# First attention of a two-block kernel: probabilities kept whole, two heads' value products side by side on TensorE

## The chip, the cores and the metric

The kernel runs as one program on one core of a Trainium2 chip. The metric is the device time of one execution in microseconds, read as the median of several runs. The core has five engines, each with its own program: TensorE (PE in the rows; its weight loads are listed apart as PEld), VectorE (DVE), ScalarE (ACT), GpSimd (POOL) and SyncE (SP, which here only issues transfers). They wait for each other through semaphores.

## The reference, cut to what matters

The reference is two transformer-like blocks on 512 rows of width 1024, all in 32-bit floats. The change lies in the attention of the first block: 8 heads, 512 queries, 768 keys (256 context rows, then 512 rows of x), 96-wide queries and keys, 64-wide values.

```python
def attend(q_nope, q_rope, k_nope, k_rope, v):
    s = (jnp.einsum('bqhd,bkhd->bhqk', q_nope, k_nope)
         + jnp.einsum('bqhr,bkr->bhqk', q_rope, k_rope)).astype(jnp.float32) * SOFTMAX_SCALE
    p = jax.nn.softmax(s, axis=-1).astype(v.dtype)
    return jnp.einsum('bqhk,bkhd->bqhd', p, v)
...
def first_block(...):
    ...
    attn_l = attend_blocked(q_nope_l, q_rope_l, ...)      # attend, 128 queries at a time
    conv_l = conformer_conv(u_l, conv_dw_w[i], conv_dw_b[i], conv_ln_g[i], conv_ln_b[i])
    y_l = merge_groups(conv_l, attn_l, w_o[i], b_o[i])    # concat, then @ w_o + b_o
    x_mid = layer_norm(ALPHA * x + g1 * y_l, ln1_g[i], ln1_b[i])
    f_l = conv_ffn(x_mid * (1 + sc2) + sh2, w_up[i], ffn_dw_w[i], ffn_dw_b[i], w_down[i], b_down[i])
    x = layer_norm(ALPHA * x_mid + g2 * f_l, ln2_g[i], ln2_b[i])
```

The second block (sparse attention, a recurrent branch, a mixture of 64 experts) follows and is the larger part of the time; the change does not touch its code.

## The kernel before, in words

**Split products.** Most products take their operands as a pair: a rounded high part (a 32-bit type that TensorE takes in one go, `F32R` in the code) and the low rest. `evac` makes such a pair out of a PSUM bank: ScalarE copies the bank into the high part (L140), then VectorE subtracts that from the bank into the low part (L141), so the second waits for the first. `mm3` multiplies two pairs with three products (L85 high by high, L86 low by high, L87 high by low). Some products, those of the experts above all, take plain 32-bit operands (`F32`) in one instruction instead; the trace records each such instruction as two.

**Before the attention.** The key-value product (`ckh`, `ckl` by `wu`) makes keys and values for six tiles of 128 rows in the two large PSUM tiles (`dbank`). ScalarE copies the keys out, and `evac` writes the values as the pair `vh`, `vl`. The query product follows, with the depthwise convolution's taps (`conv`) on VectorE and GpSimd between.

**The attention.** `items` lists (head, tile of 128 queries), head by head, 32 in all. For each item, `scores` makes a 128 by 768 score tile with six products, takes the row maximum (VectorE, L670), the exponential with its row sum (ScalarE, L673), the reciprocal (VectorE, L674), and scales the probabilities `P` on GpSimd (L675). It runs two items ahead, one score tile in each of the two `dbank`. `turn` transposes `P` on TensorE (six products with the identity, L688) into two banks, of four and of two tiles, and `evac` writes each as a pair, `PTh` and `PTl`. `values` runs for every second item, on 256 queries of one head: for each of six key tiles an `mm3` of 128 value columns (this head's 64 and those of the head beside it) by the pair of probabilities, 18 products; of the 128 rows that come out, the 64 of this head are kept (`hp`). `keys` transposes a head's queries and keys and makes pairs of them, one head ahead. From item 23 on, steps of `conv_norm` (the convolution's layer norm and its transposes, which use the same four PSUM banks) are put between.

**Order.** In this part of the program a scheduler of the compiler orders each engine's instructions from its own estimate of times; the second block's experts have a fixed order on TensorE and SyncE.

Of the kernel before, what the change touches and what calls it, by code (L numbers as in the profile page):

```python
# [9 lines left out]
F32 = mybir.dt.float32  # L10
F32R = mybir.dt.float32r
# [3 lines left out]
AF = mybir.ActivationFunctionType  # L15
# [8 lines left out]
NT = S // 128  # L24
# [36 lines left out]
class Kernel:  # L61
# [276 lines left out]
    def block1(self):  # L338
        tc, nc, io = self.tc, self.nc, self.io
        v, act, pe, pool_e = nc.vector, nc.scalar, nc.tensor, nc.gpsimd  # L340
# [229 lines left out]
        pQ_cm, pQ = op("pQ", side="right")  # L570
        k96 = pQ.tile([128, 6, 8, 96], F32, name="k96")
        q96 = pQ.tile([128, NT, 8, 96], F32, name="q96")
        vh = pQ.tile([128, 6, 512], F32R, name="vh")
        vl = pQ.tile([128, 6, 512], F32R, name="vl")
        for t in range(6):
            pool_e.tensor_scalar(k96[:, t, :, 64:96], krow[:, t:t + 1, :].to_broadcast([128, 8, 32]), 1.0, 1.0,
                                 op0=ALU.mult, op1=ALU.mult)
# [1 line left out]
        for t in range(6):  # L579
            ps = self.dbank()  # L580
            sl = slice(t * 128, (t + 1) * 128)
            for h in range(2):
                for k in range(2):
                    self.mm3(ps[:, h * 512:(h + 1) * 512], (ckh[:, k, sl], ckl[:, k, sl]),
                             (wu[0][:, k, h * 512:(h + 1) * 512], wu[1][:, k, h * 512:(h + 1) * 512]), k == 0, k == 1)
            pr = ps.rearrange("p (h c) -> p h c", h=8)
            act.activation(k96[:, t, :, 0:64], pr[:, :, 0:64], AF.Copy)
            self.evac(vh[:, t, :].rearrange("p (h c) -> p h c", h=8), vl[:, t, :].rearrange("p (h c) -> p h c", h=8),
                      pr[:, :, 64:128])
            go(conv, 4)  # L590
        wuq = [self.wblock(io["w_uq"][0], 0, 3, h * 384, 384) for h in range(2)]
        for t in range(NT):
            sl = slice(t * 128, (t + 1) * 128)
            for h in range(2):
# [4 lines left out]
                pr = ps[:, :384].rearrange("p (h c) -> p h c", h=4)  # L599
# [10 lines left out]
        atth = pK.tile([128, 4, S], F32R, name="atth")  # L610
        attl = pK.tile([128, 4, S], F32R, name="attl")
        pH_cm, pH = op("pH", 2, side="right")
# [12 lines left out]
        def conv_norm():  # L625
            cnt = pH.tile([128, NT, 512], F32, name="cnt", tag="cnt", bufs=1)
            for t in range(NT):
                ps = self.bank()
                for c in range(4):
                    pe.transpose(ps[:, c * 128:(c + 1) * 128], cacc[:, c, t * 128:(t + 1) * 128], self.ident)  # L630
                s, b, _ = self.ln_stats([ps], LN_EPS)
                act.activation(cnt[:, t, :], ps, AF.Identity, bias=b, scale=s)
                yield
            for c in range(4):
                ps = self.bank()
                for t in range(NT):
                    pe.transpose(ps[:, t * 128:(t + 1) * 128], cnt[:, t, c * 128:(c + 1) * 128], self.ident)
                sl = pH.tile([128, S], F32, name="sl")
                act.activation(sl, ps, AF.Silu, bias=col["conv_ln_b"][:, c:c + 1], scale=col["conv_ln_g"][:, c:c + 1])
                self.split(cath[:, c, :], catl[:, c, :], sl)  # L640
                yield
        tail = conv_norm()
        items = [(h, t) for h in range(8) for t in range(NT)]
        QK, PT, Pt = {}, {}, {}

        def keys(h):
            r = []
            for src, name, n in ((q96, "q", 4), (k96, "k", 6)):
                hi = pH.tile([96, 128 * n], F32R, name=name + "Th")
                lo = pH.tile([96, 128 * n], F32R, name=name + "Tl")  # L650
                for g in range(0, n, 4):
                    m = min(4, n - g)
                    ps = self.bank()
                    for t in range(m):
                        pe.transpose(ps[:96, t * 128:(t + 1) * 128], src[:, g + t, h, :], self.ident)
                    self.evac(hi[:, g * 128:(g + m) * 128], lo[:, g * 128:(g + m) * 128], ps[:96, :m * 128])
                r.append((hi, lo))
            QK[h] = r

        def scores(i):  # L660
            if i >= len(items):
                return
            h, t = items[i]
            (qTh, qTl), (kTh, kTl) = QK[h]
            ps = self.dbank()
            qsl = slice(t * 128, (t + 1) * 128)
            for c0, c1 in ((0, 512), (512, 768)):
                self.mm3(ps[:, c0:c1], (qTh[:, qsl], qTl[:, qsl]), (kTh[:, c0:c1], kTl[:, c0:c1]), True, True)
            mx = self.small.tile([128, 3], F32, name="mx")
            v.tensor_reduce(mx[:, 0:1], ps[:, :768], axis=AX.X, op=ALU.max)  # L670
            v.tensor_scalar(mx[:, 0:1], mx[:, 0:1], -MLA_SCALE, None, op0=ALU.mult)
            P = pP.tile([128, 768], F32, name="P")
            act.activation(P, ps[:, :768], AF.Exp, bias=mx[:, 0:1], scale=MLA_SCALE, accum_out=mx[:, 1:2])  # L673
            v.reciprocal(mx[:, 2:3], mx[:, 1:2])  # L674
            pool_e.tensor_scalar(P, P, mx[:, 2:3], 1.0, op0=ALU.mult, op1=ALU.mult)  # L675
            Pt[i] = P

        def turn(i):
            h, t = items[i]
            if t % 2 == 0:  # L680
                PT[h, t // 2] = [pH.tile([128, 6, 256], F32R, name="PT" + x) for x in "hl"]
            PTh, PTl = PT[h, t // 2]
            P = Pt.pop(i)
            ql = slice((t % 2) * 128, (t % 2 + 1) * 128)
            for g, n in ((0, 4), (4, 2)):
                pt = self.bank()
                for j in range(n):
                    pe.transpose(pt[:, j * 128:(j + 1) * 128], P[:, (g + j) * 128:(g + j + 1) * 128], self.ident)  # L688
                self.evac(PTh[:, g:g + n, ql], PTl[:, g:g + n, ql], pt[:, :n * 128].rearrange("p (t c) -> p t c", t=n))

        def values(i):
            h, t = items[i]
            if t % 2 == 0:
                return
            PTh, PTl = PT.pop((h, t // 2))
            vs = slice((h // 2) * 128, (h // 2) * 128 + 128)
            hp = slice((h % 2) * 64, (h % 2) * 64 + 64)
            c = slice((t // 2) * 256, (t // 2 + 1) * 256)
            po = self.bank()
            for j in range(6):  # L700
                self.mm3(po[:, :256], (vh[:, j, vs], vl[:, j, vs]), (PTh[:, j, :], PTl[:, j, :]), j == 0, j == 5)
            self.evac(atth[hp, h // 2, c], attl[hp, h // 2, c], po[hp, :256])

        keys(0)
        for i in range(2):
            scores(i)
        for i in range(len(items)):
            h, t = items[i]
            if t == 0 and h < 7:
                keys(h + 1)  # L710
            scores(i + 2)
            turn(i)
            go(conv, 3)
            if i:
                values(i - 1)
            if i >= 23:
                go(tail, 1)
        values(len(items) - 1)
        self.dump2("cath", cath, catl)
        self.dump2("catA", atth, attl)  # L720
# [23 lines left out]
        for n in range(2):  # L744
            c = slice(n * 512, (n + 1) * 512)
# [22 lines left out]
        for t in range(NT):  # L768
# [5 lines left out]
            for n in range(2):  # L774
                c = slice(n * 512, (n + 1) * 512)
# [79 lines left out]
        for c in range(11):  # L855
# [5 lines left out]
            for mm in range(2):  # L861
                j = 2 * c + mm
# [7 lines left out]
        hh, hl = self.hh, self.hl  # L870
# [23 lines left out]
        for t in range(NT):  # L894
# [4 lines left out]
            for n in range(2):  # L899
                c = slice(n * 512, (n + 1) * 512)  # L900
# [1453 lines left out]
```

## Time and profile before

| | us |
|---|---|
| median of 3 runs (lowest, highest) | 2093.3 (2086.33, 2097.59) |
| the profiled execution's own time | 2086.47 |
| its span (first to last instruction) | 2084.7 |
| TensorE busy in the span | 1918.0 (92%) |
| attention, first transpose to the end of the last value product | 243.0 to about 357.3 |
| TensorE busy from 243 to 358 | 104.2 of 115 |

The profiled execution lies 6.8 us below the median of the runs. Busy time is the union of an engine's instructions; "granted clock" is the share of TensorE's full clock that the chip let through.

### The profile page before, as it was taken

The numbers are of one execution on the slowest core, as the hardware profiler recorded it, in microseconds if no ns is written. First come the engines' busy times: TensorE is split into PE (matmuls) and PEld (weight loads), VectorE is DVE, ScalarE is ACT, GpSimd is POOL, SyncE is SP. The second block draws the span as 40 slices with busy tenths as digits, with TensorE's granted clock in tenths as the row PEclk, the third lists the DMA queues.
The fourth block names the chain that finished last, engine by engine and source line by source line (L and its number), as shares of the span: only waits on it lengthen the run. The fifth ranks groups of instructions, "written<-read, shape, count | busy, mean of one in ns | idle before, by whom it ended". The sixth has DMA issues, their size and how long they took to land.

```text
span 2084.7 us, 30137 instructions
## 1 busy us (share of the span) xinstructions
PE 1918.0 (92%) x11420; PEld 1461.2 (70%) x11427; DVE 1175.3 (56%) x2137; ACT 661.3 (32%) x1168; POOL 555.2 (27%) x448
## 2 busy tenths in 40 slices
PE   4978898979999998997899999999899999999993
PEld 2657786777777887875677877788676666767662
DVE  4896576588574468565897576667332332222223
ACT  3213466434333325544323245523111111111111
POOL 1279422352012432012002100143122322223222
PEclk8989899989999999999799999999899999999997
DMA  8651102378462223549767631553999999999895
GB/s 284 215 185 60 51 1 78 110 253 296 141 208 97 101 91 115 153 127 236 223 177 177 170 114 62 172 166 133 358 327 360 306 381 329 354 362 336 316 367 173
DMA packets 208751, 425.47 MB, mean 204 GB/s; under 512 B 46694, under 2 KB 140280, under 8 KB 182485
## 3 DMA queue, kind: packets, MB, share of 16 engines
q1 hardware_dynamic: 184914, 366.98, 50.6%
q0 software_dynamic: 15488, 39.41, 7.7%
q10 hardware_dynamic: 8195, 17.06, 2.2%
q8 instruction: 92, 1.51, 0.3%
q14 instruction: 62, 0.51, 0.1%
HBM read 375.37 MB, written 60.08 MB: 209 GB/s over the span
## 4 chain that ended last, share of the span: by engine, by line
PE 70%; DVE 10%; DMA 7%; issue 5%; ACT 3%; POOL 3%; SPq 1%; POOLq 0%; ACTq 0%; DVEq 0%
PE bank L85 10%; PE bank L87 10%; PE bank L86 10%; PE gbank L2146 9%; PE wbank L2201 6%; PE bank L2132 3%; PE bank L2109 2%; PE gbank L2157 2%; PE dbank L85 2%; PE dbank L87 2%; PE dbank L86 2%; DVE cacc L486 1%; DMA ysum_db<-y,idxr 1%; DVE wlo L81 1%; PE wbank L2190 1%
## 5 line engine op out<-in xcount | busy, mean ns | idle before, releaser
L81 DVE TENSOR_TENSOR wlo<-raw,whi 128x1024 fp32r<-128x1024 f32 (+2 forms) x163 | 221.0, 1376 | 111.5 <-ACT whi L80 107.6
L85 PE MATMUL bank<-hh,whi 128*128 128x512 f32 (+3 forms) x720 | 273.2, 383 | 3.5 <-DVE hh L163 3.0
L86 PE MATMUL bank<-hl,whi 128*128 128x512 f32 (+3 forms) x720 | 273.4, 381 | 1.5 <-DVE hl L164 1.5
L87 PE MATMUL bank<-hh,wlo 128*128 128x512 f32 (+3 forms) x720 | 273.1, 382 | 1.0 <-DVE wlo L81 1.0
L80 ACT ACTIVATE whi<-raw 128x1024 fp32r<-128x1024 f32 (+2 forms) x163 | 161.7, 1025 | 241.9 <-PE bank L86 175.9
L2146 PE MATMUL gbank<-wr,xt 128*128 128x256 f32 x928 | 210.5, 385 | 0.9 <-issue 0.3
L2146 PEld LDWEIGHTS gbank<-wr,xt 128*128 128x128 f32 x928 | 175.7, 192 | 24.9 <-ACT xt L2115 1.0
L87 PEld LDWEIGHTS bank<-hh,wlo 128*128 128x128 f32 (+2 forms) x720 | 137.0, 191 | 35.3 <-issue 3.9
L85 PEld LDWEIGHTS bank<-hh,whi 128*128 128x128 f32 (+2 forms) x720 | 137.2, 192 | 32.1 <-DVE hh L163 3.4
L86 PEld LDWEIGHTS bank<-hl,whi 128*128 128x128 f32 (+2 forms) x720 | 137.7, 191 | 29.3 <-DVE hl L164 2.3
L2201 PE MATMUL wbank<-wr,ht 128*128 128x512 f32 (+2 forms) x456 | 138.7, 599 | 6.6 <-ACT ht L2173 5.6
L2162 DVE TENSOR_TENSOR h<-gbank,h 128x256 f32<-128x256 f32 (+1 forms) x40 | 17.0, 426 | 217.0 <-ACT h L2161 217.0
L2183 DVE SCALAR_TENSOR_TENSOR y<-wbank,wt,g2l 128x512 f32<-128x512 f32 (+1 forms) x69 | 51.7, 750 | 129.6 <-PE wbank L2201 110.3
L2201 PEld LDWEIGHTS wbank<-wr,ht 128*128 128x128 f32 (+2 forms) x456 | 51.2, 154 | 73.1 <-issue 62.8
L866 POOL TENSOR_TENSOR hid<-ug,uv 128x512 f32<-128x512 f32 x22 | 36.1, 1643 | 181.3 <-DVE uv L850 181.3
L486 DVE SCALAR_TENSOR_TENSOR cacc<-vpad,cols,cacc 128x512 f32<-128x512 f32 x90 | 83.6, 968 | 0.4
L2161 ACT ACTIVATE h<-gbank 128x256 f32<-128x256 f32 (+1 forms) x40 | 15.2, 381 | 210.8 <-PE gbank L2146 174.8
L2098 POOL DMA_INDIRECT xg<-h_d,idx x40 | 41.1, 1028 | 129.8 <-DVE idx L2093 80.2
L621 POOL TENSOR_TENSOR raw<-raw,g2row 128x2048 f32<-128x2048 f32 x11 | 55.0, 4999 | 73.8 <-DMA raw<-in_w_down_dram 73.5
L2132 PE MATMUL bank<-wr,xt 128*32 128x256 f32 (+1 forms) x896 | 65.9, 381 | 0.7 <-ACT xt L2115 0.2
L1990 POOL DMA_INDIRECT ysum_da<-y,idx x21 | 32.8, 1560 | 118.6 <-DVE y L2183 86.1
L2109 PEld LDWEIGHTS bank<-ident,xg 128*128 128x128 f32 (+1 forms) x392 | 48.8, 195 | 20.3 <-issue 15.3
(692 smaller groups left out, 4263.5 us busy)
## 6 DMA issues: line engine op xcount, KB each, us to landing
wr<-in_exp_gate_dram SPq DMA_DIRECT2D x52, 1024.0 KB
wr<-in_exp_up_dram SPq DMA_DIRECT2D x52, 1024.0 KB
wr<-in_exp_down_dram SPq DMA_DIRECT2D x52, 1024.0 KB
raw<-in_w_in_dram SPq DMA_DIRECT2D x58, 512.0 KB
mraw<-in_w_ada_dram SPq DMA_DIRECT2D x24, 1024.0 KB
mraw<-in_ada_w_dram SPq DMA_DIRECT2D x24, 1024.0 KB
raw<-in_w_up_dram SPq DMA_DIRECT2D x22, 1024.0 KB
raw<-in_w_down_dram SPq DMA_DIRECT2D x11, 1024.0 KB
```

Source lines behind the costliest of these rows:

```text
L80: self.nc.scalar.activation(hi, src, AF.Copy)
L81: self.nc.vector.tensor_tensor(lo, src, hi.bitcast(F32), op=ALU.subtract)
L85: mm(out, a[0], b[0], start=start, stop=False, skip_group_check=True)
L86: mm(out, a[0], b[1], start=False, stop=False, skip_group_check=True)
L87: mm(out, a[1], b[0], start=False, stop=stop, skip_group_check=True)
L486: eng.scalar_tensor_tensor(cacc[:, c, :], vpad[:, c, i:i + S], cw[:, i * 4 + c:i * 4 + c + 1], cacc[:, c, :], op0=ALU.mult, op1=ALU.add)
L621: return lambda raw, k, n: pool_e.tensor_tensor(raw, raw, row.unsqueeze(1).to_broadcast([128, k, n]), op=ALU.mult)
L2109: pe.transpose(ps[:, k * 128:k * 128 + r], x.rearrange("s (p k) -> s k p", k=8)[0:r, 4 * g + k, :], self.ident[0:r, 0:r])
L2132: pe.matmul(ps[to, 0:256], job.xt[:, k, sl], x[:, k * 256:(k + 1) * 256], start=k == 0, stop=k == 7, skip_group_check=True)
L2146: pe.matmul(ps[:, m * 256:(m + 1) * 256], job.xt[:, k, :], w[m][:, k * 256:(k + 1) * 256], start=k == 0, stop=k == 7, skip_group_check=True)
L2183: end = lambda c, ps: v.scalar_tensor_tensor(y[r, c], ps, job.wt[r], g2row[r, c], op0=ALU.mult, op1=ALU.mult)
L2201: pe.matmul(ps[to], job.ht[:, k, sl], x[:, k * D + c.start:k * D + c.stop], start=k == 0, stop=k == 1, skip_group_check=True)
```

## The change

The probabilities are no longer split. `turn` copies each transposed bank once into a 32-bit tile `PT`: ScalarE the bank of four tiles, VectorE the bank of two. The values stay whole too (`vals` in place of `vh`, `vl`, copied by VectorE alone). `items` now goes by pairs of heads: two query tiles of the even head, the same two of the odd head, then the other two of each. `values` runs once for a pair of heads and 256 queries: for each key tile one 32-bit product per head, in turns, with the even head's 64 value columns writing the result's rows 0 to 63 and the odd head's rows 64 to 127. One `evac` of 128 rows follows where there were two of 64. `keys` of the next two heads come at the fifth and seventh of a pair's eight items.

```diff
-        vh = pQ.tile([128, 6, 512], F32R, name="vh")
-        vl = pQ.tile([128, 6, 512], F32R, name="vl")
+        vals = pQ.tile([128, 6, 512], F32, name="vals")
...
-            self.evac(vh[:, t, :].rearrange("p (h c) -> p h c", h=8), vl[:, t, :].rearrange("p (h c) -> p h c", h=8),
-                      pr[:, :, 64:128])
+            v.tensor_copy(vals[:, t, :].rearrange("p (h c) -> p h c", h=8), pr[:, :, 64:128])
...
-        items = [(h, t) for h in range(8) for t in range(NT)]
+        items = [(2 * p + h, 2 * g + t) for p in range(4) for g in range(2) for h in range(2) for t in range(2)]
...
             if t % 2 == 0:
-                PT[h, t // 2] = [pH.tile([128, 6, 256], F32R, name="PT" + x) for x in "hl"]
-            PTh, PTl = PT[h, t // 2]
+                PT[h, t // 2] = pH.tile([128, 6, 256], F32, name="PT", bufs=4)
+            to = PT[h, t // 2]
...
-                self.evac(PTh[:, g:g + n, ql], PTl[:, g:g + n, ql], pt[:, :n * 128].rearrange("p (t c) -> p t c", t=n))
+                p3 = pt[:, :n * 128].rearrange("p (t c) -> p t c", t=n)
+                if g:
+                    v.tensor_copy(to[:, g:g + n, ql], p3)
+                else:
+                    act.activation(to[:, g:g + n, ql], p3, AF.Copy)
...
-            if t % 2 == 0:
+            if t % 2 == 0 or h % 2 == 0:
                 return
-            PTh, PTl = PT.pop((h, t // 2))
-            vs = slice((h // 2) * 128, (h // 2) * 128 + 128)
-            hp = slice((h % 2) * 64, (h % 2) * 64 + 64)
+            pair = [(x, PT.pop((x, t // 2)), slice((x % 2) * 64, (x % 2) * 64 + 64)) for x in (h - 1, h)]
             c = slice((t // 2) * 256, (t // 2 + 1) * 256)
             po = self.bank()
             for j in range(6):
-                self.mm3(po[:, :256], (vh[:, j, vs], vl[:, j, vs]), (PTh[:, j, :], PTl[:, j, :]), j == 0, j == 5)
-            self.evac(atth[hp, h // 2, c], attl[hp, h // 2, c], po[hp, :256])
+                for g, p, hp in pair:
+                    pe.matmul(po[hp, :256], vals[:, j, g * 64:(g + 1) * 64], p[:, j, :], start=j == 0, stop=j == 5,
+                              skip_group_check=True)
+            self.evac(atth[:, h // 2, c], attl[:, h // 2, c], po[:, :256])
...
+        keys(1)
         for i in range(len(items)):
-            h, t = items[i]
-            if t == 0 and h < 7:
-                keys(h + 1)
+            if i % 8 in (4, 6) and i < 24:
+                keys(2 * (i // 8) + 2 + (i % 8) // 6)
```

How the instructions move, on TensorE, at the first value product of before and the second of the changed kernel (numbers after names tell tiles apart). Before, after the last transposes of a turn:

```order
L688 MATMUL bank_1885<-ident_72,P_1817 128x128 x4
L688 MATMUL bank_1892<-ident_72,P_1817 128x128 x2
L85 MATMUL bank_1902<-PTh_1821,vh_1361 128x256
L86 MATMUL bank_1902<-PTl_1822,vh_1361 128x256
L87 MATMUL bank_1902<-PTh_1821,vl_1362 128x256
```

The three products come six times (18 rows). In the changed kernel, L687 is the transpose and L704 the value product:

```order
L687 MATMUL bank_2108<-ident_72,P_2044 128x128 x4
L687 MATMUL bank_2114<-ident_72,P_2044 128x128 x2
L704 MATMUL bank_2121<-PT_1953,vals_1361 64x256
L704 MATMUL bank_2121<-PT_2048,vals_1361 64x256
L704 MATMUL bank_2121<-PT_1953,vals_1361 64x256
```

The two heads' products alternate, 12 rows in all; there are 8 such groups where there were 16 of 18.

On VectorE, at the evacuation of the first values (L520 scales the latent rows `cn` of the last query tile, and waits for GpSimd), one piece of the difference:

```order
 L81 TENSOR_TENSOR wlo<-raw,whi 128x128
 L141 TENSOR_TENSOR cql<-bank,cqh 128x3x128
+L587 COPY vals<-dbank 128x512
 L520 SCALAR_TENSOR_TENSOR cn<-bank,ss,qg 128x384
-L141 TENSOR_TENSOR vl<-dbank,vh 128x512 x2
+L587 COPY vals<-dbank 128x512 x2
 L141 TENSOR_TENSOR cql<-bank,cqh 128x3x128
```

The first copy out of a `dbank` now stands ahead of `cn`, where both stood behind it.

On TensorE at the same place, before: the key-value product of the second tile ends, and the transposes of `cn` (L541) and a query product come next.

```order
L86 MATMUL dbank_1399<-wlo_1372,ckh_774 128x512
L87 MATMUL dbank_1399<-whi_1371,ckl_775 128x512
L541 MATMUL bank_1348<-ident_72,cn_1329 128x128 x3
L85 MATMUL bank_1525<-whi_1511,cqh_776 128x384
L86 MATMUL bank_1525<-wlo_1512,cqh_776 128x384
```

In the changed kernel the 12 products of the third tile (`dbank_1418`) come ahead of those transposes; the last three of them and what follows:

```order
L85 MATMUL dbank_1418<-whi_1370,ckh_774 128x512
L86 MATMUL dbank_1418<-wlo_1371,ckh_774 128x512
L87 MATMUL dbank_1418<-whi_1370,ckl_775 128x512
L541 MATMUL bank_1348<-ident_72,cn_1329 128x128 x3
L85 MATMUL bank_1518<-whi_1504,cqh_776 128x384
```

So the transposes of `cn` and the nine query products behind them moved back by one tile's 12 products. Smaller moves of the same kind go on through the rest of the first block, among them the order in which SyncE issues the loads of `w_up` and of the second block's `ada_w`.

## Rows read from the trace of the kernel before

**Rows 1.** The page: span, and each engine's busy time, share and instructions.
```profile
span 2084.7 us, 30137 instructions
PE 1918.0 (92%) x11420; PEld 1461.2 (70%) x11427; DVE 1175.3 (56%) x2137; ACT 661.3 (32%) x1168; POOL 555.2 (27%) x448
```
**Rows 2.** Stretches: length, busy us by engine, granted clock, DMA share, GB/s.
```profile
243.00:358.00 115.00, 104.20 (x736) 93.16 (x734) 83.03 (x203) 77.70 (x170) 32.92 (x35) 0.98 0.06 19
260.00:280.00 20.00, 19.94 (x146) 18.03 (x145) 15.92 (x39) 14.08 (x34) 5.44 (x6) 1.00 0.00 1
317.00:340.00 23.00, 19.30 (x141) 17.02 (x139) 17.70 (x54) 15.35 (x33) 8.04 (x11) 1.00 0.10 30
340.00:358.00 18.00, 13.18 (x85) 11.45 (x85) 7.78 (x16) 11.85 (x23) 1.35 (x2) 0.91 0.25 80
```
**Rows 3.** Timeline of one value group, first and last of 18 products, then a transpose.
```profile
249.29 0.36 PE L85 MATMUL bank<-PTh,vh 128*128 128x256 f32 x1
...
251.40 0.28 PE L87 MATMUL bank<-PTh,vl 128*128 128x256 f32 x1
251.52 0.27 PE L688 MATMUL bank<-ident,P 128*128 128x128 f32 x1
```
**Rows 4.** Plain 32-bit products in the experts: groups by shape, then a timeline.
```profile
L2146 PE MATMUL gbank<-wr,xt 128*128 128x256 f32 x928 | 210.5, 385 | 0.9 <-issue 0.3 <-ACT xt L2115 0.2
L2157 PE MATMUL gbank<-wr,xt 128*64 128x256 f32 x352 | 40.4, 382 | 0.0
...
1495.46 3.67 PE L2157 MATMUL gbank<-wr,xt 128*64 128x256 f32 x32
1499.07 0.50 PE L85 MATMUL wbank<-sdh,shh 128*128 128x512 f32 x1
```
**Rows 5.** Groups by shape, 243 to 357: busy us, mean ns, idle before, releaser.
```profile
L141 DVE TENSOR_TENSOR PTl<-bank,PTh 128x512 fp32r<-128x512 f32 x32 | 21.9, 683 | 5.7 <-ACT PTh L140 5.7
L140 ACT ACTIVATE PTh<-bank 128x512 fp32r<-128x512 f32 x32 | 19.0, 594 | 10.1 <-PE bank L688 9.5
L141 DVE TENSOR_TENSOR PTl<-bank,PTh 128x256 fp32r<-128x256 f32 x32 | 13.2, 413 | 0.7 <-ACT PTh L140 0.7
L140 ACT ACTIVATE PTh<-bank 128x256 fp32r<-128x256 f32 x32 | 12.2, 382 | 1.5 <-PE bank L688 1.4
L141 DVE TENSOR_TENSOR attl<-bank,atth 64x256 fp32r<-64x256 f32 x15 | 6.3, 422 | 14.0 <-ACT atth L140 14.0
```
**Rows 6.** Plain VectorE copy out of PSUM, groups by shape, whole program.
```profile
L2113 DVE COPY xt<-bank 128x512 f32<-128x512 f32 x38 | 25.8, 686 | 10.0 <-PE bank L2109 8.3
```
**Rows 7.** What TensorE waited for from 243 to 357: us in total, times, longest.
```profile
PE bank L85 <- DVE PTl L141: 2.8, 4, 1.3
...
PE bank L688 <- DVE PTl L141: 0.5, 1, 0.5
```
**Rows 8.** Timeline at the last `cn`, each engine's own.
```profile
196.06 0.62 DVE L520 SCALAR_TENSOR_TENSOR cn<-bank,ss,qg 128x384 f32<-128x384 f32 x1 [2.86 <-POOL ss L124]
...
196.83 0.52 PE L541 MATMUL bank<-ident,cn 128*128 128x128 f32 x3 [2.51 <-DVE cn L520]
...
197.90 0.52 PE L85 MATMUL bank<-whi,cqh 128*128 128x384 f32 x1
198.22 0.52 PE L86 MATMUL bank<-wlo,cqh 128*128 128x384 f32 x1
```
**Rows 9.** The stretch behind that wait, columns as in group 2.
```profile
196.90:199.80 2.90, 2.90 (x12) 2.90 (x13) 1.53 (x3) 0.49 (x1) 2.62 (x4) 0.60 0.00 0
```
**Rows 10.** Stretches behind the attention, columns as in group 2.
```profile
420.00:440.00 20.00, 9.94 (x72) 8.77 (x70) 16.54 (x10) 7.14 (x17) 17.91 (x9) 0.74 0.51 186
460.00:500.00 40.00, 39.81 (x175) 30.07 (x175) 38.00 (x32) 16.16 (x21) 13.71 (x5) 1.00 0.91 315
600.00:650.00 50.00, 50.00 (x215) 37.62 (x210) 27.27 (x30) 17.50 (x22) 6.45 (x5) 1.00 0.37 119
1600.00:1800.00 200.00, 197.70 (x1367) 132.70 (x1367) 59.65 (x152) 24.96 (x57) 56.14 (x43) 1.00 0.98 343
```

## The prediction

> **What bounds the kernel now.** I read the page first, then the stretches, then the waits, then timelines. TensorE is busy 92% of the span and no other engine over 56% [rows 1], so a change is worth what it takes off TensorE, or off a wait of TensorE. The stretches say where. From 243 to 358, the attention, TensorE is busy 104.2 of 115 us: 10.8 us are idle, almost none in the steady middle (19.94 of 20), 3.7 of 23 where the convolution's norm joins in, 4.8 of 18 at the end [rows 2]. So in the middle the products themselves set the pace, and from 317 on waits do as well. Behind the attention TensorE is again busy from end to end for most of the time (39.81 of 40, 50.00 of 50, 197.70 of 200) [rows 10], and the loads there are issued as buffers come free, not at fixed times. What the attention ends earlier, the kernel should end earlier.
>
> **Value products: the main term.** Before, a group is 18 products. The first starts at 249.29 and the transpose behind the last at 251.52: 2.23 us, and 16 groups make 35.7 us [rows 3]. The changed kernel has 8 groups of 12 plain 32-bit products, 64 rows out by 256 columns, in turns on two halves of the array. The attention of before has none of these, but the experts do, in the same shape and also in turns on rows 0 to 63 and 64 to 127 of one bank: 16 of them (32 records) run from 1495.46 to 1499.07, 3.61 us, 0.226 us each, the step into the group and out of it included [rows 4]. Twelve take 2.71 us, eight groups 21.7 us. That is 14.0 us less.
>
> The other bound is a product that finds no partner: with 128 rows out the same shape takes 210.5 / 928 = 0.227 us a record, two records a product, 0.454 us [rows 4]. The paired shape gives 40.4 / 352 = 0.115 a record, half of it. So without overlap the groups would take 96 x 0.454 = 43.6 us, 7.9 more than now. I take 21.7: the rows of the paired shape are the change's own shape, down to the bank. The one difference is that there both halves are given the same 64 columns as weights, here different ones; they are loaded anew for each product there too.
>
> The Trainium skill speaks against the change here: "FP8 and Floating Point Precision", section "TensorE Precision Notes", says a true 32-bit product goes through the array four times, against the three products of a split one, and "TensorEngine Tiling (Array Packing)", section "Key Properties", that a change of tiling mode drains the engine. By four passes alone a group would be an estimated 12 x 4 x 256 columns at 2.4 GHz, 5.1 us against 2.23. The same section says that tiles work independently, and the trace agrees with that half: 0.115 us a record where two alternate. The drain is inside the 3.61 us.
>
> **Evacuations.** The transposed banks lose 32 ScalarE copies of 382 ns (12.2 us) and 32 VectorE subtractions of 683 ns (21.9 us). The subtraction of two tiles, 413 ns, becomes a copy [rows 5]; a plain copy of a full bank takes 686 ns [rows 6], as much as the subtraction's 683, so I price it at 413 still. The result's evacuations halve (422 ns on VectorE [rows 5], 8 fewer, 3.4 us). VectorE goes from 83.0 to about 58 us of work in this stretch, ScalarE from 77.7 to about 62. Neither set the pace, so this counts only through waits. TensorE's waits for the low parts were 2.8 and 0.5 us [rows 7], and the part that is waited for no longer exists. I take 2 us (bounds 0 and 3.3).
>
> **The place before the attention.** VectorE stood waiting for GpSimd with `cn` (2.86 us), the copies out of both `dbank` queued behind it, and TensorE stood 2.51 us for `cn` [rows 8]. Behind the wait the granted clock was 0.60, between the levels of 1.2 and 2.4 GHz [rows 9], and the nine query products were 0.32 us apart [rows 8]; at the upper level they would take half, so this cost another 9 x 0.16 = 1.4 us. In the changed order one copy stands ahead of `cn`, its `dbank` comes free, and twelve products of the next tile fill TensorE's wait. Fully hidden that is 3.9 us. I take 3.5; the lower bound is 0, should the copy not be there in time.
>
> **New waits.** With less to do, TensorE's work from 243 on falls from 104.2 to about 90 us, and the chain of an item (maximum, exponential, reciprocal, scaling, transposes, copy) must fit under it at the same depth of two items. The values of a pair wait for four turns in place of two. Where the chain already shows, from 317 to 340, TensorE idles 3.7 of 23 us, 16% [rows 2]. At that share throughout, 90 us of work would take 107, where 90 and the present 10.8 idle make 101: 6 us more. Zero is the other bound, since VectorE and ScalarE are relieved. I take half, 3 us. The two heads' `keys` come two items before use, as before, and their buffers were last read an item earlier on TensorE's own queue, so I count nothing for them; the one stretch that hides them is the steady middle, and if it did not, their wait is in the 6 us.
>
> **Moves behind the attention** (order of loads and of VectorE's work up to about 800 us): no more instructions than before, TensorE full there [rows 10]. I count 0, with 5 us to either side: VectorE is busy 38.0 of 40 us from 460 to 500, so a load or a sum moved there can be late, and TensorE stands half of 420 to 440 (9.94 of 20), where a better order could win.
>
> **Sum.** -14.0 - 2 - 3.5 + 3 = -16.5 us: the profiled execution's 2086.5 becomes 2070.0. That execution lies 6.8 us below the median of the runs, so against 2093.3 I predict 2076.8, 0.8% less.
>
> **Rivals.**
> - *The products of two heads do not overlap* (slower). The groups cost 43.6 us, +7.9; with -2 and -3.5 and TensorE again the only pace (no new waits) that is +2.4: 2095.7. It decides from 0.372 us a product on (35.7 / 96); the paired rows' 0.226 speak against it. This is where the skill's four passes would lead.
> - *The chain of an item becomes the pace.* If TensorE idles 20% of the stretch, as between the 16% of 317 to 340 and the 27% of 340 to 358 [rows 2], 90 us of work take 112.5: 2.5 won there, with the 3.5 ahead of it 6 us, 2087.3. For it: the middle is free of idle only because the products were long. Against: VectorE, on whose low parts and maxima most of these waits end, loses 25 of 83 us.
> - *The gain is given back behind.* If the moved loads or sums cost 5 us in the stretch that is full on VectorE, 2082; with both bounds against me 2086.
> - *The place before the attention does not gain:* 2080.3, still the forecast's own range.
>
> **How the numbers follow.** The forecast, 2068 to 2083, has 62%; the chain 20%; given back behind 10%; no overlap 6%; better than 2068 2%. What can be told from no change here is about 0.5%, 10.5 us (the three runs spread over 11 us), so faster means below 2082.8, slower above 2103.8. Faster: the forecast, the better case and a small part of the giving back, 0.66. Slower needs no overlap together with new waits, or something not seen: 0.05. Same: 0.29. The range, 2067 to 2091, reaches over the chain's 2087 and the bound of the giving back, and leaves out the case without overlap.
>
> **What would show it.** The 12 products of a group span about 2.7 us, records 0.115 us apart; 5.4 us would prove the first rival. The stretch from the first transpose to the last value product shrinks from 114 to about 99 us, with TensorE idle 10 to 14 of it; idle of 20 or more, released by the maximum, the exponential or the scaled `P`, is the second. The transposes of the last `cn` should follow products without a gap, at full clock, and the attention start about 4 us earlier. VectorE should be near 58 us in the attention. Behind it, the distance from the last value product to the end should stay as it is within 5 us; if it grows by more, the third rival holds.

## The result, and the profile after

The changed kernel takes 2065.4 us in the median of six runs (2059.97 to 2070.51); six runs of the kernel before have a median of 2092.4. The ratio is 0.9868, with an interval of 0.9843 to 0.9893: 1.3% faster, about 27 us, where 16.5 were forecast. The time lies 1.6 us below the range. The profiled execution took 2060.43 us, 26.0 less than that of before. First its page, which answers to [rows 1]:

```profile
span 2058.5 us, 29821 instructions
PE 1902.5 (92%) x11331; PEld 1436.4 (70%) x11331; DVE 1161.6 (56%) x2097; ACT 648.3 (31%) x1124; POOL 558.0 (27%) x448
```

TensorE lost 15.5 us of busy time, the span 26.2. To see where, the program is cut at three points that both kernels have: the transposes of the second last `cn` (A begins), the end of the last query product (A ends, B begins), and the end of the last value product (B ends, C begins). The stretches A, B and C of before, with the columns of [rows 2]:

```profile
188.36:226.59 38.23, 33.60 (x153) 29.61 (x152) 15.34 (x44) 13.03 (x28) 24.65 (x37) 0.91 0.06 16
226.59:357.24 130.65, 115.21 (x785) 102.00 (x782) 91.07 (x223) 84.24 (x182) 40.84 (x41) 0.95 0.11 37
357.24:2084.70 1727.46, 1628.65 (x9756) 1230.11 (x9762) 927.14 (x1636) 514.91 (x874) 398.30 (x279) 0.96 0.66 221
```

and of the changed kernel:

```profile
184.39:216.28 31.89, 30.26 (x153) 26.65 (x152) 16.87 (x44) 9.99 (x22) 25.49 (x37) 1.00 0.07 19
216.28:327.49 111.21, 98.59 (x689) 78.66 (x686) 70.36 (x183) 71.38 (x142) 40.81 (x41) 0.95 0.13 43
327.49:2058.50 1731.01, 1633.50 (x9763) 1232.23 (x9762) 933.51 (x1636) 517.71 (x876) 400.48 (x279) 0.96 0.66 221
```

The first numbers of the lines give the ledger: 3.97 us ahead before A begins, 6.34 won in A, 19.44 in B, 3.55 lost in C; together 26.2.

**B, the attention.** One value group in the timeline, beside [rows 3]:

```profile
278.89 2.81 PE L704 MATMUL bank<-PT,vals 128*64 128x256 f32 x24
281.63 0.33 PE L687 MATMUL bank<-ident,P 128*128 128x128 f32 x1
```

From the group's start to the next transpose it is 2.74 us (2.71 forecast), in 24 records 0.114 us apart. Seven of the eight take 2.74 or 2.75. The groups by shape from 217 to 328, beside [rows 5]:

```profile
L704 PE MATMUL bank<-PT,vals 128*64 128x256 f32 x192 | 23.0, 384 | 0.7 <-ACT PT L692 0.5 <-ACT sl L637 0.2
L692 ACT ACTIVATE PT<-bank 128x512 f32<-128x512 f32 x32 | 19.0, 597 | 11.0 <-PE bank L687 11.0
L690 DVE COPY PT<-bank 128x256 f32<-128x256 f32 x32 | 13.3, 417 | 4.7 <-PE bank L687 4.7
L141 DVE TENSOR_TENSOR attl<-bank,atth 128x256 fp32r<-128x256 f32 x8 | 3.4, 424 | 8.1 <-ACT atth L140 8.1
```

The copy of two tiles costs what the subtraction did (417 ns against 413), as priced. What TensorE waits for in the same stretch, beside [rows 7] (us, times, longest):

```profile
PE dbank L85 <- ACT P L672: 5.5, 2, 4.5
PE bank L687 <- ACT PT L692: 2.0, 3, 0.7
PE bank L635 <- ACT sl L637: 1.2, 1, 1.2
```

No wait on the maximum is among them, and GpSimd's scaling holds TensorE once, for 0.7 us. The longest, 4.5 us, lies ahead of the first transpose and is there in the kernel before as well. TensorE idles 12.6 us in B, 15.4 before. From the first transpose on, beside the attention's row in [rows 2]:

```profile
230.90:327.49 96.59, 89.64 (x644) 71.60 (x644) 62.52 (x165) 64.14 (x128) 34.62 (x36) 0.98 0.07 23
```

That is 96.6 us where it was 114.2, with TensorE idle for 6.9. The prediction named about 99 (its own terms for this stretch, -14, -2 and +3, make 101) and 10 to 14 idle; idle of 20 or more, its sign for the second rival, did not come. VectorE has 62.5 us of work there, not 58.

The two B differ in the clock as well. In before, TensorE's longest wait for a low part (1.3 us [rows 7]) ends at 340.71, and behind it the granted clock is at the lower of its two levels, 1.2 GHz:

```profile
341.00:344.00 3.00, 3.00 (x15) 3.00 (x15) 0.16 (x1) 0.76 (x3) 0.91 (x1) 0.50 1.07 345
```

The value group that begins there takes 3.76 us, 1.5 more than the clean ones (2.26). In the changed kernel the clock is at 1.00 from 236 to the end of B.

**A, the place before the attention.** Its last `cn` and what follows on TensorE, beside [rows 8]:

```profile
192.10 0.62 DVE L520 SCALAR_TENSOR_TENSOR cn<-bank,ss,qg 128x384 f32<-128x384 f32 x1 [2.21 <-POOL ss L124]
192.91 0.49 PE L541 MATMUL bank<-ident,cn 128*128 128x128 f32 x3
193.15 0.42 PE L85 MATMUL bank<-whi,cqh 128*128 128x384 f32 x1
193.41 0.34 PE L86 MATMUL bank<-wlo,cqh 128*128 128x384 f32 x1
193.59 0.34 PE L87 MATMUL bank<-whi,cql 128*128 128x384 f32 x1
```

VectorE still waits for GpSimd (2.21 us), but TensorE does not wait for `cn` any more, and the products behind it are 0.18 us apart, not 0.32. A has a second place of this kind, which the prediction did not look at: TensorE's wait for the weights of the query product, and the products behind it. In before, that wait and what follows it:

```profile
211.00:213.53 2.53, 0.41 (x3) 0.01 (x1) 0.72 (x2) 2.08 (x4) 0.55 (x1) 1.00 0.00 0
213.53:218.17 4.64, 4.64 (x17) 4.64 (x18) 1.40 (x2) 0.52 (x2) 0.00 (x0) 0.63 0.00 0
```

and in the changed kernel:

```profile
203.00:204.80 1.80, 0.17 (x2) 0.01 (x1) 0.72 (x2) 1.60 (x3) 1.62 (x3) 1.00 0.00 0
204.80:209.40 4.60, 4.60 (x26) 4.60 (x27) 2.92 (x2) 0.91 (x3) 2.69 (x2) 1.00 0.00 0
```

Behind a wait of 2.12 us (in the timeline) the granted clock was 0.63 in the mean, and 17 records took 4.64 us. Behind 1.63 us it stayed at 1.00, and 26 records took 4.60. The means of 0.60 [rows 9] and 0.63 each mix the two levels; inside both stretches of before the clock is at the lower one, 1.2 GHz:

```profile
198.00:200.00 2.00, 2.00 (x8) 2.00 (x7) 0.47 (x1) 0.00 (x0) 1.82 (x3) 0.50 0.00 0
215.00:217.00 2.00, 2.00 (x8) 2.00 (x7) 0.00 (x0) 0.38 (x1) 0.00 (x0) 0.50 0.00 0
```

So A's 6.3 us are 3.0 of idle time (4.63 before, which is 2.51 and 2.12; 1.63 after) and 3.3 of products at the lower clock (33.60 us busy against 30.26, for 153 records in both).

### The profile page after: what moved, and what is told of

The parts are those of the page before. It is cut to its first block, busy times and chain, and to the rows that moved or that the text cites. A ratio compares the mean times of both kernels' runs of the same rounds, so it can differ in the third digit from the quotient of the medians.

```text
span 2058.5 us, 29821 instructions
## 1 busy us (share of the span) xinstructions
PE 1902.5 (92%) x11331; PEld 1436.4 (70%) x11331; DVE 1161.6 (56%) x2097; ACT 648.3 (31%) x1124; POOL 558.0 (27%) x448
## 4 chain that ended last, share of the span: by engine, by line
PE 70%; DVE 9%; DMA 7%; issue 5%; ACT 3%; POOL 3%; SPq 1%; ACTq 0%; POOLq 0%; DVEq 0%
PE bank L85 10%; PE bank L86 10%; PE bank L87 10%; PE gbank L2151 9%; PE wbank L2206 6%; PE bank L2137 3%; PE bank L2114 2%; PE dbank L85 2%; PE gbank L2162 2%; PE dbank L87 2%; PE dbank L86 2%; DVE wlo L81 2%; DVE cacc L486 1%; PE bank L704 1%; DMA ysum_db<-y,idxr 1%
## 5 line engine op out<-in xcount | busy, mean ns | idle before, releaser
L2166 ACT ACTIVATE h<-gbank 128x256 f32<-128x256 f32 (+1 forms) x40 | 15.2, 381 | 209.7 <-PE gbank L2151 173.7
```

## The experiments

In all of them the stretches A, B and C are cut at the same three points. The time of a whole run moves by 10 to 30 us between executions of one kernel; the stretches A and B, as the repeat shows, by 0.03 us.

**The values copied once, in the kernel before (e1 and e1b).**

```diff
-            self.evac(vh[:, t, :].rearrange("p (h c) -> p h c", h=8), vl[:, t, :].rearrange("p (h c) -> p h c", h=8),
-                      pr[:, :, 64:128])
+            v.tensor_copy(vh[:, t, :].rearrange("p (h c) -> p h c", h=8), pr[:, :, 64:128])
```

In e1 the third product took `vh` for `vl`; in e1b it takes a tile of zeros.

> The kernel before, with one edit: the values are copied once, by VectorE, as in the change; their low part is left out and its products take the high part again, so TensorE has as many products as before. VectorE then has one such copy ahead of cn and TensorE twelve products of the next tile in its wait, as in the changed kernel. If the place before the attention is worth what the two traces differ by there (6.3 us from the transposes of the second last cn to the last query product, TensorE's wait and the slow clock behind it and behind the next wait), this gains about 6 us against 2092.4: 2086. If it is worth the 3.5 us of the prediction: 2089. If it is worth nothing and the lead was chance: 2092. In the trace the stretch from the transposes of the second last cn to the last query product (41.5 us before, 35.2 after) tells which; the attention itself stays at 114 us.

> The kernel before with the values copied once, by VectorE; their low part is left out (a tile of zeros stands in its place, so that TensorE has as many products). Unlike in e1 the result stays close to the reference's, and the experts get the same rows. By the stretches that e1 and e2 showed (from the transposes of the second last cn to the last query product 38.2 us or 31.9, from there to the first transpose 16.4 or 14.6) the place before the attention is worth 8.1 us: 2084.6 against 2092.7. By the prediction's 3.5: 2089. If the lead is given back behind: 2092.

e1 took 2309.2 us. Taking the high part twice doubles the values, so other rows go to the experts: their products on 256 columns (928 before) are 992. Its time says nothing on the change, but A and B lie ahead of the experts:

```profile
187.97:219.87 31.90, 30.27 (x153) 26.64 (x152) 16.93 (x44) 10.00 (x22) 25.56 (x37) 1.00 0.06 19
219.87:349.53 129.66, 114.36 (x784) 101.38 (x782) 91.04 (x223) 84.56 (x182) 40.94 (x41) 0.95 0.11 37
```

e1b, with the experts' rows as before, has the same A and B and a median of 2090.25 us, ratio 0.9981 (0.9962 to 0.9999):

```profile
187.13:219.10 31.97, 30.34 (x153) 26.58 (x152) 15.66 (x44) 10.19 (x23) 25.86 (x37) 1.00 0.07 19
219.10:348.77 129.67, 114.43 (x784) 101.49 (x782) 90.92 (x223) 84.43 (x182) 40.81 (x41) 0.95 0.11 37
```

So the one copy in place of a copy and a subtraction brings all of A's 6.3 us, and 1.0 in B. The 8.1 us expected were a little too many: in e1b's B the first transpose comes 2.0 us earlier than before, and 1.0 of that is lost again behind it. The gain of the whole run, 0.2 to 8 us by its interval, holds 7.2 as well as the prediction's 3.5.

**The pair of instructions for the values, in the changed kernel (e2).** The edit is that of e1 the other way round; VectorE's result is read by nothing.

```diff
-            v.tensor_copy(vals[:, t, :].rearrange("p (h c) -> p h c", h=8), pr[:, :, 64:128])
+            self.evac(vals[:, t, :].rearrange("p (h c) -> p h c", h=8), vrest[:, t, :].rearrange("p (h c) -> p h c", h=8),
+                      pr[:, :, 64:128])
```

> The changed kernel, with one edit: the values are written as in the kernel before, by a copy on ScalarE and a subtraction on VectorE (whose result nothing reads), so both copies out of the two dbank stand behind cn again. If the place before the attention is worth about 6 us, this loses 6 against 2065.4: 2071.5, and TensorE waits some 2.5 us for cn at a slow clock behind it. By the prediction's 3.5: 2069. If the place is worth nothing: 2065.

```profile
188.09:226.31 38.22, 33.59 (x153) 29.55 (x152) 15.34 (x44) 13.04 (x28) 24.74 (x37) 0.91 0.06 16
226.31:336.78 110.47, 99.31 (x689) 79.06 (x686) 70.47 (x183) 71.19 (x142) 40.94 (x41) 0.95 0.13 44
```

A is back at 38.2 us with a clock of 0.91, B is unchanged within 0.7. The median is 2077.6 us, ratio 0.9921 (0.9893 to 0.9950). By the ratios that is a loss of 11 us against the changed kernel, where A and B explain 5.6; two such intervals leave some 8 us to either side of it, so they don't settle whether anything was lost beyond A (the clock, under "Moves behind the attention", bears on it).

**The same products in sequence (e3).**

```diff
-            for j in range(6):
-                for g, p, hp in pair:
+            for g, p, hp in pair:
+                for j in range(6):
```

> The changed kernel with the same products in another order: six of the even head, then six of the odd head, instead of in turns. If two products overlap only where neighbours lie on different columns of the array, a group takes about 12 x 0.454 = 5.4 us in place of 2.74, 8 groups 21.6 us more: 2087. If the overlap does not hang on the order, or a product of 64 columns costs half anyway: 2065, groups of 2.7 us.

```profile
286.69 4.59 PE L704 MATMUL bank<-PT,vals 128*64 128x256 f32 x24
291.21 0.55 PE L687 MATMUL bank<-ident,P 128*128 128x128 f32 x3
```

A group takes 4.52 us, 0.377 a product in the mean, against 0.228 in turns. The mean mixes two prices. The 24 records of that group in order of time, eight by eight:

```profile
286.69 1.94 PE L704 MATMUL bank<-PT,vals 128*64 128x256 f32 x8
288.46 1.08 PE L704 MATMUL bank<-PT,vals 128*64 128x256 f32 x8
289.38 1.89 PE L704 MATMUL bank<-PT,vals 128*64 128x256 f32 x8
```

Alone on one half of the array, eight records take 1.89 us (1.94 with the step into the group), as long as eight of 128 columns in e5. Only at the switch from one head to the other, where records of both meet, do eight take 1.08, as in turns. So the overlap hangs on the order, and a product of 64 columns without a partner costs as much as one of 128. B:

```profile
217.22:340.42 123.20, 110.10 (x677) 86.42 (x677) 69.66 (x182) 71.58 (x142) 40.77 (x41) 0.96 0.12 39
```

That is 12.0 us more than in the changed kernel, where the groups alone account for 8 x 1.78 = 14.2; the time is 2077.2 us, ratio 0.9942 (0.9913 to 0.9971). I had expected 21.6, from 0.454 us a product and without the overlap at the switch.

**Whole probabilities without pairs (e5).** The kernel before with `PT` and `vals` whole and six products of 128 columns for a head:

```diff
-                self.mm3(po[:, :256], (vh[:, j, vs], vl[:, j, vs]), (PTh[:, j, :], PTl[:, j, :]), j == 0, j == 5)
+                pe.matmul(po[:, :256], vals[:, j, vs], p[:, j, :], start=j == 0, stop=j == 5, skip_group_check=True)
```

> The kernel before with whole probabilities and values but without pairs of heads: six plain 32-bit products of 128 columns for a head and 256 queries, 16 groups, order of items and keys as before, each transposed bank copied once. Prediction's price of an unpaired product is 0.454 us: groups of 2.72 us, 43.6 us in all, 7.9 (against 37 measured as 6.5) more than before. With the place before the attention (-6) and the lighter evacuations and waits (-2 to -4) it comes out 0 to 2 us below before: 2091. If the gain of the change came from the evacuations and waits and not from the pairs, it is nearer to the changed kernel: 2070 to 2080. If waits for an item's chain appear with whole heads in order: above 2095.

```profile
282.52 2.75 PE L703 MATMUL bank<-PT,vals 128*128 128x256 f32 x12
283.38 1.89 PE L703 MATMUL bank<-PT,vals 128*128 128x256 f32 x8
285.11 0.38 PE L686 MATMUL bank<-ident,P 128*128 128x128 f32 x2
```

The second line is the group's last eight records by themselves. A group takes 2.59 us (some 2.69), 0.432 a product; 16 of them 41.4. The Trainium skill, "FP8 and Floating Point Precision", section "TensorE Precision Notes", has four passes for such a product, an estimated 4 x 256 columns at 2.4 GHz, 0.427 us; the trace agrees here, and with two on different columns it shows 0.228 for each, as "TensorEngine Tiling (Array Packing)", "Key Properties", has it of tiles that work independently. B:

```profile
219.39:348.80 129.41, 117.37 (x688) 101.24 (x686) 75.04 (x191) 75.62 (x150) 40.92 (x41) 0.96 0.12 37
```

The products cost 16 x (2.59 - 2.26) = 5.3 us more than the split ones, yet B is as long as in e1b (129.67). The lighter evacuations gave these 5.3 us back: TensorE idles 12.0 us in B for 15.2 in e1b, and a stretch at the lower clock that e1b has late in B (0.50 from 333 to 335) is not there. The time is 2078.55 us, ratio 0.9937 (0.9916 to 0.9958), below the 2091 expected.

**The low parts made again, in the changed kernel (e6).**

```diff
-                if g:
-                    v.tensor_copy(to[:, g:g + n, ql], p3)
-                else:
-                    act.activation(to[:, g:g + n, ql], p3, AF.Copy)
+                act.activation(to[:, g:g + n, ql], p3, AF.Copy)
+                rest = pH.tile([128, 512], F32, name="rest")
+                v.tensor_tensor(rest[:, :n * 128].rearrange("p (t c) -> p t c", t=n), p3, to[:, g:g + n, ql], op=ALU.subtract)
```

> The changed kernel with the low parts of the probabilities made again (ScalarE copies both banks, VectorE subtracts; nothing reads the result), products as in the change. VectorE gets about 22 us more in the attention, ScalarE 12. If the fall of TensorE's idle time in the attention from 10.0 to 6.9 us came from the missing low parts, about 3 us come back: first transpose to last value product 99.7 in place of 96.6, 2068.5. If it came from elsewhere: 2065.4. If with shorter value products VectorE's evacuations become the pace (the prediction's chain): 8 us or more, 2073.

```profile
218.33:337.46 119.13, 101.86 (x688) 80.98 (x686) 87.86 (x215) 79.93 (x174) 40.79 (x41) 0.94 0.13 41
```

B grows by 7.9 us, 4.7 of it idle and 3.3 busy, with value groups of 2.74 us as in the change; the time is 2076.6 us, ratio 0.9919 (0.9888 to 0.9949). In the middle of the attention TensorE of this kernel is busy 18.4 of 20 us, and VectorE 16.7 to 17.0:

```profile
250.00:270.00 20.00, 18.38 (x134) 15.20 (x131) 17.04 (x40) 14.60 (x34) 5.29 (x6) 1.00 0.00 1
270.00:290.00 20.00, 18.41 (x138) 14.78 (x136) 16.67 (x39) 13.71 (x32) 5.57 (x7) 1.00 0.00 1
```

**The copies on one engine (e8, e9).** In e8 ScalarE copies both transposed banks of the changed kernel, in e9 VectorE does. Of the four lines of `turn` that e6 takes out, one stays, for e8 and for e9:

```diff
+                act.activation(to[:, g:g + n, ql], p3, AF.Copy)
```

```diff
+                v.tensor_copy(to[:, g:g + n, ql], p3)
```

> The changed kernel with both transposed banks copied by ScalarE (in the change: four tiles ScalarE, two tiles VectorE). 13.3 us of copies go from VectorE to ScalarE: VectorE from 70.4 to about 57 us between the last query product and the last value product, ScalarE from 71.4 to about 83.6. If VectorE's work is what the chain of an item is held by (e6: 17.5 us more on VectorE and 8.6 on ScalarE made that stretch 7.9 us longer), the stretch of 111.2 us gets shorter, 108 to 110. If ScalarE's is (it carries the exponentials, and TensorE waits 2.5 us for its copies), it gets longer, by 2 to 6: 113 to 117. If only the sum of both counts: 111. The time follows the stretch: 2062 to 2072.

> The changed kernel with both transposed banks copied by VectorE: 32 copies of 0.69 us go there (22 us), 32 of 0.60 leave ScalarE (19 us): VectorE about 92 us, as much as in the kernel before (91), ScalarE 52. If VectorE's work is what holds the chain, the stretch from the last query product to the last value product is as long as in e6 or longer (119 to 123 against 111.2), 2073 to 2077. If ScalarE's copy is, it gets shorter than 111. If it is the handing over from ScalarE's copy to VectorE's subtraction that cost the time in e6, which is not there here: 111 to 113.

B of e8:

```profile
217.52:331.62 114.10, 101.68 (x688) 80.25 (x686) 60.23 (x151) 79.09 (x174) 40.77 (x41) 0.94 0.13 42
```

and of e9:

```profile
218.40:337.33 118.93, 103.03 (x689) 80.75 (x686) 86.69 (x215) 56.22 (x110) 40.87 (x41) 0.94 0.12 41
```

With ScalarE at 79 us B is 2.9 us longer than in the change, with VectorE at 87 it is 7.7 longer, as in e6, though nothing is handed from ScalarE to VectorE here. e8 came out where it was expected if ScalarE held the chain (113 to 117), e9 just under where it was expected if VectorE did (119 to 123). So work on either engine counts, 10 us less of it on VectorE (60 for 70) won nothing, and the change's share between the two is the best of the three in B. Whether it is the amount of work, or that the two copies of a turn no longer run side by side on two engines, was not tried apart. e8 also has e6's copies on ScalarE without its subtractions: of e6's 7.9 us, 2.9 come with these copies, and the subtractions add the other 5.0. The times are 2078.4 us (ratio 0.9913, 0.9883 to 0.9944) and 2074.1 us (0.9890, 0.9846 to 0.9934).

**GpSimd's scaling of w_o later (e7).** A try at a better kernel: the two scalings are issued in the loop, behind the scaled `P` of a later item.

```diff
-        w_first = [self.wload(w_o, 0, 4, n * 512, 512, gated(g1row[:, n * 512:(n + 1) * 512])) for n in range(2)]
+        w_first = [self.wload(w_o, 0, 4, n * 512, 512) for n in range(2)]
...
+            if i in (8, 16):
+                raw, n, f = w_first[i // 16]
+                with tc.issue_after(self.scaled):
+                    gated(g1row[:, (i // 16) * 512:(i // 16 + 1) * 512])(f(raw), 4, 512)
```

> The changed kernel with GpSimd's two scalings of w_o (4.55 us each) put behind the scaled probabilities of the items 10 and 18, instead of ahead of the first and third. In the changed kernel the first P is ready at 226.2 and is scaled at 230.0, behind the first of them. If that wait sets the start of the attention, the first transpose comes 3.8 us earlier: 2061.6. If the items behind are held by the maximum or the exponential anyway, or the scalings now delay a later P: 2065.4 or more.

```profile
217.17:325.99 108.82, 97.00 (x688) 77.48 (x686) 70.24 (x183) 71.69 (x142) 40.98 (x41) 0.97 0.13 44
```

The first transpose was expected 3.8 us earlier; it comes 0.9 us earlier (13.7 us after the last query product for 14.6), so the wait behind the first scaling sets little of the start. B is 2.4 us shorter, 1.6 of it in TensorE's busy time, at a granted clock of 0.97 for 0.95. The time, 2071.8 us (2056.97 to 2079.74), ratio 0.9884 (0.9851 to 0.9918), does not tell this kernel from the changed one.

**The changed kernel once more (r_after).**

> The changed kernel once more, without an edit: how far its stretches move from one profiled execution to another. If the early lead (first transpose of cn at 127.2 against 130.5) is chance, it moves by some us here; the stretches from the second last cn to the last query product (31.9), to the first transpose (14.6) and to the last value product (96.6) should repeat to within 0.5 us, and the distance from there to the end (1701.7) shows how much of the 3.3 us given back is chance. The time: 2065.

```profile
188.02:219.94 31.92, 30.29 (x153) 26.66 (x152) 16.91 (x44) 10.00 (x22) 25.57 (x37) 1.00 0.07 19
219.94:331.17 111.23, 98.59 (x689) 78.64 (x686) 70.37 (x183) 71.43 (x142) 40.93 (x41) 0.95 0.13 43
331.17:2073.80 1742.63, 1641.42 (x9763) 1238.18 (x9762) 934.16 (x1636) 518.09 (x876) 404.26 (x279) 0.95 0.66 219
```

A and B repeat to 0.03 us. A begins at 188.02, not 184.39, and C is 11.6 us longer, in one and the same kernel. The median, 2067.2 us, and the ratio, 0.9866 (0.9842 to 0.9889), repeat. Of the 11.6 us in C, 7.9 are TensorE's busy time for the same 9763 records, at a mean granted clock of 0.95 in place of 0.96; 3.7 are idle. One of the places that differ is a transfer that TensorE waits for (`q` of the second block), in C of the repeat:

```profile
PE bank L1159 <- DMA q<-q_d: 7.0, 2, 6.6
```

and in C of the first profile of the changed kernel:

```profile
PE bank L1159 <- DMA q<-q_d: 5.9, 2, 3.8
```

## Why the prediction fell short

The direction and the main term were right. What repeats from run to run, A and B, is 6.3 + 19.4 = 25.8 us, where the prediction had 3.5 + 13 = 16.5. The median moved by 27. Of the 9.3 us between them, 2.8 lie in A; in B the products' 14.2 leave 5.2 us of gain for everything else, where the evacuations and the new waits had been put at +1 together.

- **Value products, -14.0.** Right. Groups of 2.74 us for 2.71, 8 x 2.74 = 21.9 us against 16 x 2.26 = 36.2 in the clean groups of before: 14.2. The first rival (43.6 us) is out for products in turns, and e3 shows the condition: with the same products in sequence the groups take 8 x 4.52 = 36.2 us, no less than the split ones, and a product without a partner costs 0.432 us.
- **Evacuations, -2.** This is the first step that failed. It priced the low parts by the waits that name them [rows 7], 3.3 us in all. Put back under the short products they cost 7.9 us (e6; 2.9 of it with the copies on ScalarE, by e8), and taken away under the long ones of e5 they pay for 5.3 us of longer products. A part of what the named waits left out is in the trace of before. Behind the longest of them the clock fell, and one value group took 1.5 us more (B, above). The prediction had reckoned slow products behind the wait for `cn`, but none behind these waits. Why the named waits were too few beyond that is only argued: VectorE's subtractions and maxima stand in one queue, so what delays a maximum shows as a wait for `P` later.
- **New waits, +3.** It was added beside the evacuations as if they were independent. With the low parts still made, B takes 119.1 us (e6), so the shorter products win 11.5 of their 14.2 us against before, and 10.5 against e1b, which like e6 has the values copied once: 2.7 to 3.7 us of new waits, the size that I took (the order of the items differs too). Without the low parts they do not appear: TensorE's idle time falls by 2.8 us. So an item's chain does cost time when VectorE has 87 us of work in B (e6, e9), and the change leaves it 70. The two terms together came to about -5 (-4 if 1.0 in B belongs to the values' copy, as in e1b), not +1.
- **The place before the attention, -3.5.** The mechanism was right, the size was not: 6.3 us in A (e1, e1b, e2), and 1.0 in B (e1b). The wait of 2.5 us and 1.4 us for the nine query products at the slow clock were counted. The prediction stopped there, and left out the first products of the next tile, still slow, and the second wait, for the query weights: 0.5 us longer before than after, with its own slow stretch behind it. The slow products of both places cost 3.3 us, not 1.4.
- **Moves behind the attention, 0 with 5 to either side.** Not settled. C came out 3.55 us longer, but by 11.6 us more in a second profile of the same kernel, so this kind of row can't tell a few us behind the attention. By the ratios some of the edited kernels lost more in the whole than in A and B (e2 about 6 us more, e8 about 7), others less (e5 about 4, e9 about 3); the ratios' intervals are as wide as that, so no loss behind is shown for any of them. A difference that the runs do show is the clock: the mean granted clock of the executions is 0.957 for the changed kernel and 0.955 in its repeat, 0.949 for e2 and 0.950 for e8, and within a kernel a lower clock goes with a longer time (in the repeat 2075.58 us at 0.949, 2063.33 at 0.959). What lowers it there was not tried.
- **The 4.0 us ahead of A** belong to no step of the change. Over the twelve profiled executions A begins between 184.4 and 188.4, and the repeat of the changed kernel has 188.02.

The range reached too little to the low side. Its lower end came from 2% for "better than the forecast", though the evacuations and the place were bounded by what single rows named, and both errors had the same sign.

## What to carry to other kernels

What an engine's relief is worth is not the sum of the waits that name it now: price it against the pace after the change, when the cover is shorter, and together with the term for new waits. The price of a stall goes on to the end of the slow products behind it and to the next wait in line, so add up a stretch from its start to the next point where both kernels do the same. Products of half width share the array only with a neighbour on the other half, so issue them in turns. In a program of this length compare profiles by stretches that repeat, and find out by a second profile which do.

## What the runs showed of the hardware

- A plain 32-bit product on 256 columns of data took 0.432 us, with 128 weight columns (e5) and also with 64 when its neighbours lay on the same half of the array (e3). In turns on the two halves, products of 64 weight columns ran two at a time, 0.228 us each with the step into and out of the group.
- After TensorE had stood for 2.51 and 2.12 us, its granted clock was at 0.50, the lower level, in the stretches from 198 to 200 and from 215 to 217, and back at 1.00 from 201 and from 218; after 1.63 us in the second place it stayed at 1.00.
